# Letting a build-time scheduler choose the engine for copies, ReLUs, squares and adds, with the VectorE/GpSimd port in its clock

## The chip, the cores and the metric

The kernel runs on all 8 cores of one Trainium2 chip, each core working on 2 of the 16 sequences. The metric is the device time of the slowest core, in microseconds (us). A program on all 8 cores has a second, slower state in some executions, in which one die shows a lower granted TensorE clock; only fast runs are compared here. A ratio is the mean time of one kernel's fast runs over the mean of the fast runs of the kernel before, taken in the same rounds on the same chip. It is therefore not quite the ratio of the medians that are also quoted.

Engine names: PE is TensorE, DVE is VectorE, ACT is ScalarE, POOL is GpSimd, SP is SyncE.

## The reference

Two layers over a (16, 2048, 1024) stream. Layer 0 mixes with retention (6 heads of 128), layer 1 with causal forgetting attention (12 heads of 64). Both add 4 heads of attention to 256 memory tokens, an output projection, and a squared-ReLU MLP, each between two RMS norms.

```python
def reference(x, mem, ...):                       # cut to its structure
    for i in range(2):
        h = rmsnorm(x, g_pre_mix[i])
        proj = h @ w_in[i]                        # q | k | v | (gate or forget logits) | memory-q
        self_out = retention(...) if i == 0 else forgetting_attention(...)
        mem_out = memory_attention(mq, mem, g_mem[i], w_mem_kv[i])
        x = x + rmsnorm(concatenate([self_out, mem_out], -1) @ w_out[i], g_post_mix[i])
        h = rmsnorm(x, g_pre_mlp[i])
        u = relu(h @ w_up[i])
        x = x + rmsnorm((u * u) @ w_down[i], g_post_mlp[i])
    return x
```

## The kernel before

The kernel is written as many small generator tasks, and a list scheduler runs once, at build time. It keeps a clock for each engine and, at each step, advances the task that can go first. So the order of every engine's instructions is fixed at build time from modelled costs, and any change to the model reorders all engines.

```python
class Sched:
    def add(self, eng, fn, reads=(), writes=(), ..., cost=100.0):
        ...                                        # cut: dependencies become semaphores
        t = self.avail[eng]
        for d in keep:
            t = max(t, d.end + HOP)                # HOP = 160 ns between engines
        op.cost = cost
        op.end = t + cost
        ...
        self.avail[eng] = op.end                   # cut: DMAs have another rule

class Tasks:
    def run(self):
        while self.live:
            now = S.avail["pe"]
            for t in self.live:                    # in order of rank
                ...
                r = S.ready(*p) + (SLACK if p[0] == "pe" else 0.0)
                if r <= now + SOON: best = t; break
                if best is None or r < best_r: best, best_r = t, r
            self.step(best)
```

The engine of each operation was written by hand. The places that the change touches (cut):

```python
def seam(...):                                     # residual add after a norm, 8 chunks
    stt(t.ap, hb.ap[:, c, :], gcol(gi, l, c), rs.ap, ALU.mult, ALU.mult, ...)          # DVE -> tb
    tt(xs[c].ap, xs[c].ap, t.ap, ALU.add, ..., eng=("pool" if c % 2 else "dve"))
def square(...):   act(sq.ap, src, AF.Square, [srcR], [sq.R])
def v_proj(...):   act(dst, o3, AF.Copy, ...) if n % 2 else cp(dst, o3, ...)           # cp is DVE
def rope(...):     tt(dst.ap, t1.ap, swp.ap, ALU.add, ..., eng="pool")                 # the rope add
def head_end(...): tt(mix[:, h, :], rs.ap, sg.ap, ALU.mult, ..., eng="pool")           # retention product
def fin(...):      tt(mix[:, p, :], o_.ap, r.ap, ALU.mult, ..., eng="pool")            # attention product
def evac(hb, oc, bk, sm):                          # after the output projection
    cp(hb.ap[:, oc, :], bk.ap, [bk.R], [hb.R[oc]])                                     # DVE
    act(sq.ap, bk.ap, AF.Square, [bk.R], [sq.R])
def mlp_job(...):
    act(r.ap, bk.ap, AF.Relu, [bk.R], [r.R])
    tt(u2[:, i, :], r.ap, r.ap, ALU.mult, [r.R], [u2R[i]])                             # u square, DVE
```

The kernel divides PSUM, the memory that matmuls write their results to, into 8 banks; 3 of them (called `G` in the code) serve all projections and the whole MLP, so the next group of 8 to 32 matmuls waits until a copy, ReLU or product has emptied one of the three.

The softmax here doesn't subtract the row's maximum and nothing guards it: scores larger than these inputs give would overflow.

## Time and profile before

| | before |
|---|---|
| median of 40 runs | 3601.12 us |
| fastest | 3589.0 us |
| PE, DVE, ACT, POOL busy | 92%, 54%, 49%, 18% |

From the page of the kernel before (slowest core, 7): busy time of each engine with its share and its count; the clock granted to PE in 40 slices, in tenths; the chain that ended last, by engine.

```profile
...
PE 3308.0 (92%) x16476; PEld 1537.4 (43%) x16476; DVE 1947.4 (54%) x3273; ACT 1773.0 (49%) x3173; POOL 661.4 (18%) x708
...
PEclk9789999999999999999999999999999999999998
...
PE 77%; DMA 7%; DVE 7%; issue 5%; ACT 3%; SPq 1%; POOL 1%; DVEq 0%; ACTq 0%; POOLq 0%
...
```

PE is the bound. Its clock dips (7 and 8 tenths) in the second and third slice and in the last. But "92% busy" contains modelled ends of matmuls, so a better reading is the spacing. The table of engine busy time in two stretches of the MLP, kernel before (from:to in us; length; then busy time and count of PE, PEld, DVE, ACT, POOL; granted clock, DMA share, GB/s):

```profile
...
3330.00:3420.00 90.00, 90.00 (x418) 40.79 (x417) 38.55 (x63) 25.07 (x42) 10.73 (x10) 1.00 0.61 193
3420.00:3510.00 90.00, 90.00 (x418) 40.83 (x417) 18.47 (x39) 22.35 (x38) 1.33 (x3) 1.00 0.38 122
...
```

418 matmuls of 512 columns in 90 us is 215 ns each, with a granted clock of 1.00: PE's full rate here. DVE and ACT are mostly idle here; there is nothing to gain in these stretches.

For the rest of this document *PE loss* means this: over all consecutive matmul starts, the spacing less what the first one's columns take at the full clock, (columns x 0.4167 + 2) ns, summed, plus the time before the first matmul and that after the last. The formula is a fit to the trace, where back-to-back matmuls start 215 to 216 ns apart at 512 columns, 162 to 163 at 384 and 56 at 128. It is worked out from the trace, as a mean over the six cores whose matmul records are complete. Stages are cut where a stage's first value-projection matmul is issued.

| PE loss, us | first block | rest of 1st retention | 1st forgetting | 2nd retention | 2nd forgetting | after the last output projection | sum |
|---|---|---|---|---|---|---|---|
| before | 112.9 | 72.7 | 86.0 | 52.8 | 44.7 | 37.8 | 407 |

The cores spread by 0.5 to 5 us in a column (standard deviation). 56 of the 407 us are matmuls that ran at half clock after a gap (427 ns apart at 512 columns); 351 us are gaps.

Groups of DVE instructions of the kernel before (line, engine, operation, names, shapes, count | busy us, mean ns | idle before, with what ended it):

```profile
...
L624 DVE TENSOR_TENSOR u_s<-rb_s 128x512 bf16<-128x512 bf16 x512 | 247.5, 484 | 507.0 <-ACT rb_s L615 506.0
...
L624 DVE TENSOR_TENSOR xt_s<-xt_s,tb_s 128x512 f32<-128x512 f32 x128 | 121.7, 950 | 28.1 <-DVE tb_s L627 11.4 <-DMA xt_s<-xs 10.7
L636 DVE CAST hb_s<-pb 128x512 bf16<-128x512 f32 x144 | 99.2, 690 | 128.3 <-PE pb L604 127.5
...
L624 DVE TENSOR_TENSOR un_s<-pb,un_s 128x512 f32<-128x512 f32 x96 | 65.9, 687 | 35.1 <-PE pb L604 31.5 <-DMA un_s<-rot 2.7
...
```

The residual add (`xt_s<-xt_s,tb_s`) averages 950 ns, while operations of the same 512 columns that read PSUM (`pb`) take 687 to 690 ns. In the trace of core 7, 84 of the 128 adds have no POOL operation beside them and take 693 ns, and 44 have one and take 1443 ns on average. This lengthening beside POOL is called a *port hold*, or hold, below. The list of waits of the kernel before, all engines (waiting engine, line and tile <- releaser: us in total, times, longest):

```profile
...
ACT sq_s L615 <- DVE hb_s L636: 232.0, 134, 5.0
...
DVE un_s L636 <- DMA vcache<-un_s: 93.3, 18, 13.2
...
ACT un_s L615 <- DMA vcache<-un_s: 65.8, 12, 10.1
...
```

ACT's square of an output bank waits for DVE's copy of the same bank (232 us); copies of values wait for the store of the previous values (93 and 66 us).

### The profile page before, as it was taken

To read this page: it belongs to the slowest core of one execution; us is meant where nothing else is said; L and a number is where in the kernel's file an instruction comes from. 1 tells how busy PE (TensorE), PEld (TensorE's weight loads), DVE (VectorE), ACT (ScalarE), POOL (GpSimd) and SP (SyncE) were. 2 spreads that over 40 slices of the span, in tenths; PEclk is the share of its full clock that TensorE was granted. 3 is DMA by queue.
4 is the path that set the end of the run, shared out by engine and by line. 5 is a ranking of instruction groups with operands and counts; after the bars stand their busy time and mean duration, and the time that the engine had idled before them with its cause. 6 is when DMAs were issued, how large, how long until landed. Compare 5 with 4: busy or idle time off the path is not lost.

```text
span 3590.2 us, 57714 instructions; the slowest of 8 cores (3567.0 to 3590.2 us)
## 1 busy us (share of the span) xinstructions
PE 3308.0 (92%) x16476; PEld 1537.4 (43%) x16476; DVE 1947.4 (54%) x3273; ACT 1773.0 (49%) x3173; POOL 661.4 (18%) x708
## 2 busy tenths in 40 slices
PE   5688999898999898999999999999999989999996
PEld 2234444443444343443444444444444444444442
DVE  4666766465544534436666666666665453524514
ACT  3544444354732484874444444444575358586221
POOL 1222322111102101011222212231111101102102
PEclk9789999999999999999999999999999999999998
DMA  9779885876346848466653655355565453634534
GB/s 185 173 222 219 225 241 173 199 212 206 115 162 176 212 133 214 111 172 208 190 190 103 200 194 181 123 184 179 161 196 158 154 173 106 188 95 144 183 120 164
DMA packets 271411, 623.27 MB, mean 174 GB/s; under 512 B 54912, under 2 KB 66816, under 8 KB 271104
## 3 DMA queue, kind: packets, MB, share of 16 engines
q1 hardware_dynamic: 220928, 449.70, 39.4%
q0 software_dynamic: 50176, 169.89, 19.8%
q8 instruction: 143, 2.34, 0.3%
q14 instruction: 164, 1.34, 0.2%
HBM read 505.08 MB, written 168.56 MB: 188 GB/s over the span
## 4 chain that ended last, share of the span: by engine, by line
PE 77%; DMA 7%; DVE 7%; issue 5%; ACT 3%; SPq 1%; POOL 1%; DVEq 0%; ACTq 0%; POOLq 0%
PE pb L604 76%; DMA vcache<-un_s 2%; DMA wm_s<-wall 2%; DVE un_s L624 1%; DVE tb_s L627 1%; SPq L639 1%; ACT sq_s L615 1%; DMA wf_s<-wall 1%; DVE un_s L643 1%; DVE sq_s L624 1%; DVE xt_s L624 1%; ACT rs_s L615 1%; DMA xt_s<-xT 0%; POOL un_s L624 0%; DMA xt_s<-xs 0%
## 5 line engine op out<-in xcount | busy, mean ns | idle before, releaser
L604 PE MATMUL pb<-u_s,wf_s 128*128 128x512 bf16 x4096 | 995.4, 382 | 35.9 <-DVE un_s L636 13.7
L604 PE MATMUL pb<-hb_s,wf_s 128*128 128x512 bf16 x4096 | 966.2, 383 | 35.0 <-ACT rb_s L615 8.5
L615 ACT ACTIVATE pt_s<-pb,dcol_s 128x512 bf16<-128x512 f32 x960 | 561.4, 624 | 118.4 <-PE pb L604 99.9
L604 PEld LDWEIGHTS pb<-hb_s,wf_s 128*128 128x128 bf16 x4096 | 399.6, 99 | 513.1 <-issue 70.7
L604 PE MATMUL pb<-hb_s,wm_s 128*128 128x512 bf16 (+1 forms) x2240 | 586.4, 387 | 32.1 <-DVE un_s L624 13.1
L604 PEld LDWEIGHTS pb<-u_s,wf_s 128*128 128x128 bf16 x4096 | 396.3, 98 | 487.4 <-issue 57.7
L624 DVE TENSOR_TENSOR u_s<-rb_s 128x512 bf16<-128x512 bf16 x512 | 247.5, 484 | 507.0 <-ACT rb_s L615 506.0
L615 ACT ACTIVATE rb_s<-pb 128x512 bf16<-128x512 f32 x512 | 304.6, 596 | 439.0 <-PE pb L604 363.8
L604 PE MATMUL pb<-un_s 65*128 65x512 bf16 (+5 forms) x1536 | 405.1, 303 | 10.5 <-DVE rs_s L624 2.4
L615 ACT ACTIVATE sq_s<-xt_s 128x512 bf16<-128x512 f32 (+1 forms) x400 | 235.2, 610 | 270.9 <-DVE xt_s L624 221.5
L604 PE MATMUL pb<-pt_s,un_s 128*128 128x512 bf16 x960 | 326.9, 346 | 0.0
L604 PEld LDWEIGHTS pb<-hb_s,wm_s 128*128 128x128 bf16 (+1 forms) x2240 | 211.0, 99 | 265.4 <-issue 66.4
L624 POOL TENSOR_TENSOR xt_s<-xt_s,tb_s 128x512 f32<-128x512 f32 x128 | 178.3, 1393 | 630.5 <-DVE tb_s L627 609.7
L636 DVE CAST un_s<-pb 64x512 bf16<-64x512 f32 (+1 forms) x256 | 167.4, 654 | 232.5 <-PE pb L604 129.3
L624 DVE TENSOR_TENSOR un_s<-pb,un_s 128x512 f32<-128x512 f32 (+2 forms) x336 | 231.0, 687 | 61.9 <-PE pb L604 31.5
L615 ACT ACTIVATE sq_s<-pb 128x512 bf16<-128x512 f32 x192 | 114.6, 597 | 268.1 <-DVE hb_s L636 232.0
L604 PE MATMUL pb<-mix_s,wm_s 128*128 128x512 bf16 x1024 | 239.4, 384 | 7.7 <-ACT sq_s L615 4.6
L636 DVE COPY rs_s<-pb 64x512 f32<-64x512 f32 x192 | 132.1, 688 | 196.2 <-PE pb L604 121.1
L624 DVE TENSOR_TENSOR sq_s<-sq_s 128x512 bf16<-128x512 bf16 (+1 forms) x408 | 189.4, 477 | 80.5 <-ACT sq_s L615 77.6
L572 POOL DMA_DIRECT2D wm_s<-wbf x154 | 87.0, 565 | 773.6 <-PE pb L604 753.7
L604 PE MATMUL pb<-wm_s,hb_s 128*128 128x384 bf16 x1024 | 195.8, 337 | 25.5 <-DVE un_s L636 10.2
L627 DVE SCALAR_TENSOR_TENSOR tb_s<-hb_s,cst_s,rs_s 128x512 f32<-128x512 bf16 x256 | 196.2, 779 | 22.8 <-ACT rs_s L615 22.8
(70 smaller groups left out, 2788.5 us busy)
## 6 DMA issues: line engine op xcount, KB each, us to landing
wf_s<-wbf SPq DMA_DIRECT2D x224, 512.0 KB, 4.2
wm_s<-wbf POOLq DMA_DIRECT2D x133, 768.0 KB, 6.3
xs<-xt_s SPq DMA_DIRECT2D x192, 256.0 KB, 4.5
xt_s<-xs SPq DMA_DIRECT2D x192, 256.0 KB, 6.7
xt_s<-xT SPq DMA_DIRECT2D x128, 256.0 KB, 8.3
wf_s<-wall POOLq DMA_DIRECT2D x64, 512.0 KB, 8.3
wbf<-wf_s SPq DMA_DIRECT2D x64, 512.0 KB, 6.5
y<-xt_s SPq DMA_DIRECT2D x112, 256.0 KB, 3.7
```

What stands on the lines that cost most here:

```text
L572: S.add(self.eng, (lambda d_, s_: lambda e, sem: e.dma_start(out=d_, in_=s_).then_inc(sem, 16))(dst, src), reads=[wbR[key]], writes=[self. ...
L604: S.add("pe", lambda e: e.matmul(out, lhsT=lhsT, rhs=rhs, start=start, stop=stop, **kw), reads=reads, writes=writes, cost=c)
L615: S.add("act", lambda e: e.activation(out=out, in_=in_, func=func, **kw), reads=reads, writes=writes, cost=c + 0.833 * nfree(out))
L624: S.add(eng, lambda e: e.tensor_tensor(out=out, in0=in0, in1=in1, op=op), reads=reads, writes=writes, cost=vcost(eng, out, (in0, in1)))
L627: S.add(eng, lambda e: e.scalar_tensor_tensor(out=out, in0=in0, scalar=scalar, in1=in1, op0=op0, op1=op1), reads=reads, writes=writes, cos ...
L636: S.add(eng, lambda e: e.tensor_copy(out=out, in_=in_), reads=reads, writes=writes, cost=vcost(eng, out, (in_,)))
L639: S.add("sp", lambda e, sem: e.dma_start(out=out, in_=in_).then_inc(sem, 16), reads=reads, writes=writes, dma=True, dres=dres, nbytes=nbyt ...
L643: S.add(eng, lambda e: e.memset(ap, v), reads=reads, writes=writes, cost=100 + 0.5 * nfree(ap))
```

## The change

The intent: give each of these operations to the engine that would finish it first on the scheduler's clock. It has three parts:

- **the ACT/DVE part**: copies out of PSUM, key scaling, ReLU and squares choose between ACT and DVE;
- **the POOL part**: residual adds, rope adds, products, square adds and casts choose between DVE and POOL (casts also ACT);
- **the port part**: the scheduler's clock treats the SBUF port that DVE and POOL share as one more resource. An operation with two SBUF inputs on either, or a POOL copy, starts no earlier than the last booking ends, and the choice weighs this too.

```diff
+        self.port = 0.0
...
+        if port:
+            t = max(t, self.port)
+            self.port = t + cost
...
+    def on_chip(*ins):
+        return len(ins) > 1 and not any("psum" in str(type(i.tensor)).lower() for i in ins)
+    def either(engs, cost, reads, writes, port=()):
+        return min(engs, key=lambda e: max(S.ready(e, reads, writes), S.port if e in port else 0.0) + cost[e])
+    def evacuate(out, in_, reads, writes, engs=("dve", "act")):
+        e = either(engs, {...}, reads, writes, ("pool",))
+        ...                                        # act(... AF.Copy ...) or cp(..., eng=e)
+    def tt_any(out, in0, in1, op, reads, writes):
+        e = either(("dve", "pool"), {"dve": vcost(...), "pool": vcost(...) + POOLB}, reads, writes, ("dve", "pool"))
+        tt(out, in0, in1, op, reads, writes, eng=e)
...
-            tt(xs[c].ap, xs[c].ap, t.ap, ALU.add, ..., eng=("pool" if c % 2 else "dve"))
+            tt_any(xs[c].ap, xs[c].ap, t.ap, ALU.add, ...)
-        cp(hb.ap[:, oc, :], bk.ap, [bk.R], [hb.R[oc]])
+        evacuate(hb.ap[:, oc, :], bk.ap, [bk.R], [hb.R[oc]])
-                    act(r.ap, bk.ap, AF.Relu, [bk.R], [r.R])
+                    if either(("act", "dve"), {"act": 700.0, "dve": 800.0}, [bk.R], [r.R]) == "dve":
+                        ts(r.ap, bk.ap, 0.0, None, ALU.max, None, [bk.R], [r.R])
+                    else:
+                        act(r.ap, bk.ap, AF.Relu, [bk.R], [r.R])
...                                                # cut: fourteen more places of the same kinds, and port=... in tt, stt and cp
```

More of the change, by code (lines that the diff above doesn't have):

```diff
@@ L94, in ready, with add @@
         return t
-    def add(self, eng, fn, reads=(), writes=(), dma=False, ndma=1, dres=None, final=False, cost=100.0, nbytes=0, ncast=0):
+    def add(self, eng, fn, reads=(), writes=(), dma=False, ndma=1, dres=None, final=False, cost=100.0, nbytes=0, ncast=0, port=False):
         op = Op()
@@ L232 @@
 SOON = 60.0
+POOLB = 300.0
 class Buf:
@@ L621, in vcost, with squared @@
         return 125 + (0.62 if out.dtype == BF and all(i.dtype == BF for i in ins) else 1.1) * n
+    def on_chip(*ins):
[3 more added lines that the diff above has]
+    def evacuate(out, in_, reads, writes, engs=("dve", "act")):
+        e = either(engs, {"dve": vcost("dve", out, (in_,)), "act": 172 + 0.833 * nfree(out), "pool": vcost("pool", out, (in_,))}, reads, writes, ("pool",))
+        if e == "act":
+            act(out, in_, AF.Copy, reads, writes)
+        else:
+            cp(out, in_, reads, writes, eng=e)
+    def squared(out, in_, reads, writes):
+        if either(("act", "dve"), {"act": 700.0, "dve": 900.0}, reads, writes, ("dve",)) == "dve":
+            tt(out, in_, in_, ALU.mult, reads, writes)
+        else:
+            act(out, in_, AF.Square, reads, writes)
+    def tt_any(out, in0, in1, op, reads, writes):
+        e = either(("dve", "pool"), {"dve": vcost("dve", out, (in0, in1)), "pool": vcost("pool", out, (in0, in1)) + POOLB}, reads, writes, ("dve", "pool"))
+        tt(out, in0, in1, op, reads, writes, eng=e)
     def tt(out, in0, in1, op, reads, writes, eng="dve"):
-        S.add(eng, lambda e: e.tensor_tensor(out=out, in0=in0, in1=in1, op=op), reads=reads, writes=writes, cost=vcost(eng, out, (in0, in1)))
+        S.add(eng, lambda e: e.tensor_tensor(out=out, in0=in0, in1=in1, op=op), reads=reads, writes=writes, cost=vcost(eng, out, (in0, in1)),
+              port=on_chip(in0, in1))
     def stt(out, in0, scalar, in1, op0, op1, reads, writes, eng="dve"):
         S.add(eng, lambda e: e.scalar_tensor_tensor(out=out, in0=in0, scalar=scalar, in1=in1, op0=op0, op1=op1),
-              reads=reads, writes=writes, cost=50 + vcost(eng, out, (in0, in1, U_f)))
+              reads=reads, writes=writes, cost=50 + vcost(eng, out, (in0, in1, U_f)), port=on_chip(in0, in1))
     def ts(out, in0, s1, s2, op0, op1, reads, writes, eng="dve"):
@@ L635, in cp @@
     def cp(out, in_, reads, writes, eng="dve"):
-        S.add(eng, lambda e: e.tensor_copy(out=out, in_=in_), reads=reads, writes=writes, cost=vcost(eng, out, (in_,)))
+        S.add(eng, lambda e: e.tensor_copy(out=out, in_=in_), reads=reads, writes=writes, cost=vcost(eng, out, (in_,)), port=eng == "pool")
     def spdma(out, in_, reads, writes, dres, nbytes, **kw):
@@ L721, in sq_into @@
             a = sm.acc[sm.n % 2]
-            tt(a.ap, a.ap, sq.ap, ALU.add, [a.R, sq.R], [a.R])
+            tt_any(a.ap, a.ap, sq.ap, ALU.add, [a.R, sq.R], [a.R])
             sq.busy = False
@@ L728, in square @@
         yield ("act", [srcR], [sq.R])
-        act(sq.ap, src, AF.Square, [srcR], [sq.R])
+        squared(sq.ap, src, [srcR], [sq.R])
         if free is not None:
@@ L770, in seam @@
             stt(t.ap, hb.ap[:, c, :], gcol(gi, l, c), rs.ap, ALU.mult, ALU.mult, [hb.R[c], rs.R, cstR], [t.R])
-            tt(xs[c].ap, xs[c].ap, t.ap, ALU.add, [xs[c].R, t.R], [xs[c].R], eng=("pool" if c % 2 else "dve"))
+            tt_any(xs[c].ap, xs[c].ap, t.ap, ALU.add, [xs[c].R, t.R], [xs[c].R])
             t.busy = False
@@ L943, in mem_q @@
             yield from group(bk, lambda k: wu[u][:, k, :], lambda k: h.ap[:, k, :], lambda k: [wR, h.R[k]])
-            act(mix[:, 6 + u, :], bk.ap, AF.Copy, [bk.R], [mixR[6 + u]])
+            evacuate(mix[:, 6 + u, :], bk.ap, [bk.R], [mixR[6 + u]])
             bk.busy = False
@@ L1036, in v_proj @@
                     dst, w_ = vs.ap[:, :, 0:3:2, :], [vs.R]
-                if n % 2:
-                    act(dst, o3, AF.Copy, [bk.R], w_)
-                else:
-                    cp(dst, o3, [bk.R], w_)
+                evacuate(dst, o3, [bk.R], w_)
                 bk.busy = False
@@ L1071, in rest @@
             yield (e_, [t1.R, swp.R], [dst.R])
-            tt(dst.ap, t1.ap, swp.ap, ALU.add, [t1.R, swp.R], [dst.R], eng=e_)
+            tt_any(dst.ap, t1.ap, swp.ap, ALU.add, [t1.R, swp.R], [dst.R])
             if b == 0:
                 f0 = (qf0 if name == "q" else kf0)[hs.ap]
-                tt(f0.ap, t1.ap[:, 0:128], swp.ap[:, 0:128], ALU.add, [t1.R, swp.R], [f0.R], eng=e_)
+                tt_any(f0.ap, t1.ap[:, 0:128], swp.ap[:, 0:128], ALU.add, [t1.R, swp.R], [f0.R])
             t1.busy = False
@@ L1088, in rest @@
                 yield ("dve", [tb.R], [kt.R])
-                ts(kt.ap, tv, kd, None, ALU.mult, None, [tb.R, cstR], [kt.R])
+                if either(("dve", "act"), {"dve": 450.0, "act": 690.0}, [tb.R], [kt.R]) == "dve":
+                    ts(kt.ap, tv, kd, None, ALU.mult, None, [tb.R, cstR], [kt.R])
+                else:
+                    act(kt.ap, tv, AF.Copy, [tb.R, cstR], [kt.R], scale=kd)
                 tb.busy = False
@@ L1219, in head_end @@
             ob.busy = False
-            tt(mix[:, h, :], rs.ap, sg.ap, ALU.mult, [rs.R, sg.R], [mixR[h]], eng="pool")
+            tt_any(mix[:, h, :], rs.ap, sg.ap, ALU.mult, [rs.R, sg.R], [mixR[h]])
             rs.busy = sg.busy = False
@@ L1312, in fox_qk @@
         for hh in range(2):
-            cp(qs[hh].ap[0:64, :], bk.ap[64 * hh:64 * hh + 64, :], [bk.R], [qs[hh].R[0]])
+            evacuate(qs[hh].ap[0:64, :], bk.ap[64 * hh:64 * hh + 64, :], [bk.R], [qs[hh].R[0]])
         bk.busy = False
@@ L1327, in fox_qk @@
         for hh in range(2):
-            cp(ks[hh].ap[0:64, bsl(b)], bk.ap[64 * hh:64 * hh + 64, :], [bk.R], [ks[hh].R[b]])
+            evacuate(ks[hh].ap[0:64, bsl(b)], bk.ap[64 * hh:64 * hh + 64, :], [bk.R], [ks[hh].R[b]])
         bk.busy = False
@@ L1362, in fin @@
             act(r.ap, r.ap, AF.Exp, [r.R], [r.R], scale=-1.0)
-            tt(mix[:, p, :], o_.ap, r.ap, ALU.mult, [o_.R, r.R], [mixR[p]], eng="pool")
+            tt_any(mix[:, p, :], o_.ap, r.ap, ALU.mult, [o_.R, r.R], [mixR[p]])
             r.busy = o_.busy = False
@@ L1384, in pv @@
                         o_ = yield from rsB.acq()
-                    cp(r.ap[p0:p0 + 64, :], ob.ap[q0:q0 + 64, :], [ob.R], [r.R])
-                    cp(o_.ap[p0:p0 + 64, :], ob.ap[p0:p0 + 64, :], [ob.R], [o_.R])
+                    evacuate(r.ap[p0:p0 + 64, :], ob.ap[q0:q0 + 64, :], [ob.R], [r.R])
+                    evacuate(o_.ap[p0:p0 + 64, :], ob.ap[p0:p0 + 64, :], [ob.R], [o_.R])
                     ob.busy = False
@@ L1482, in y_part @@
         x = yield from xB.acq()
-        if t:
-            yield ("dve", [bk.R], [x.R])
-            cp(x.ap, bk.ap, [bk.R], [x.R])
-        else:
-            yield ("act", [bk.R], [x.R])
-            act(x.ap, bk.ap, AF.Copy, [bk.R], [x.R])
+        yield ("act" if S.avail["act"] < S.avail["dve"] else "dve", [bk.R], [x.R])
+        evacuate(x.ap, bk.ap, [bk.R], [x.R])
         bk.busy = False
@@ L1499, in y_whole @@
         yield ("act", [x.R], [sq.R])
-        act(sq.ap, x.ap, AF.Square, [x.R], [sq.R])
+        squared(sq.ap, x.ap, [x.R], [sq.R])
         K.spawn(sq_into(sm, sq), 0)
@@ L1503, in y_whole @@
         yield (e_, [x.R], [hb.R[oc]])
-        cp(hb.ap[:, oc, :], x.ap, [x.R], [hb.R[oc]], eng=e_)
+        evacuate(hb.ap[:, oc, :], x.ap, [x.R], [hb.R[oc]], ("dve", "act", "pool"))
         x.busy = False
@@ L1531, in mlp_job @@
                     r = yield from rB.acq()
-                    act(r.ap, bk.ap, AF.Relu, [bk.R], [r.R])
+                    if either(("act", "dve"), {"act": 700.0, "dve": 800.0}, [bk.R], [r.R]) == "dve":
+                        ts(r.ap, bk.ap, 0.0, None, ALU.max, None, [bk.R], [r.R])
+                    else:
+                        act(r.ap, bk.ap, AF.Relu, [bk.R], [r.R])
                     bk.busy = False
```

## The prediction

> **What bounds it now.** TensorE. The page's busy table gives PE 3308 us of 3590 (92%), DVE 54%, ACT 49%, POOL 18%; the chain of waits is 77% PE. In the MLP stretch at 3330-3510 us the stage table shows 418 matmuls per 90 us, 215 ns each; spacing all matmuls at that rate leaves an estimated 370 us of PE loss, 282 us of it visible as idle. Where it lies matters: about 128 us in the first 360 us, about 58 us at 360-720, about 73 us in the second retention stage (1620-2520), about 60 us in the four starts of forgetting attention (near 700, 880, 1200, 1390 us), where copies wait for the value-cache stores, and almost none in MLP stretches. By the list of waits PE waits some 215 us for DVE, ACT or POOL and 32 us for DMA; of the first, about 95 us fall before 360 us and about 63 us in the other retention stretches.
>
> **What the port costs now.** The Trainium skill, "SBUF — State Buffer", section "SBUF: two separate sides", says a VectorE operation with two SBUF inputs and a GpSimd operation exclude each other for their whole length. This trace agrees: DVE's residual add takes 693 ns (median) with no POOL operation beside it and 1443 ns (mean of 44) with one; the u square 426 and 962; copies and adds that read PSUM take 687 either way. Summed over the groups, DVE is held an estimated 120 us.
>
> **What the change does** (the instruction order shows it). POOL's arithmetic falls from 456 to 53 operations: all 128 residual adds, all 96 mix products, 84 of 96 rope adds and 87 of 112 casts leave it, most to DVE. To ACT go 136 of 144 output copies, 76 query/key copies, 39 key scalings, 37 value copies; to DVE come 99 of 512 ReLUs and 23 squares. Costed with this trace's durations (0.69 us per DVE add or PSUM copy, 0.60 per ACT copy), DVE gains about 330 us and loses about 210 us, plus about 110 us of the port holds: DVE stays near 1950 us. ACT rises by about 125 us to near 1900; POOL falls to about 200 us, mostly DMA issue.
>
> **How much is on the critical path.** Little. PE's own work is unchanged. Rope adds and mix products get shorter (1.3 to 0.7 us), holds of 0.5 to 3 us inside DVE's queue go, so retention and startup waits should shrink by about a third: (95+63)/3, about 50 us. Not helped: weight loads at startup (DMA 70-92% busy up to 540 us), value-cache stores, MLP. The seams gain nothing: a pair of chunks takes 3.0 us now (timeline of the tail); all on DVE it is 2x(0.74+0.17+0.69)=3.2 us. So the last 25 us after the last matmul stay.
>
> **Predicted:** 3545 us, range 3485 to 3605. Faster by over 2%: 0.30; within 2%: 0.66; slower by over 2%: 0.04.
>
> **What would show each step.** Residual add back at 693 ns with hardly a 1.4 us case, u square mean near 430; DVE busy 1900-2000, ACT 1850-1950, POOL 150-250; PE busy about the same, PE idle 220-250; the gain before 720 us and in 1620-2520, none in MLP stretches; value-cache waits still there.
>
> **What would make it wrong.** Startup waits that are really DMA-bound leave only 20 us; ACT queues during forgetting attention (already 80 of 90 us busy at 1260-1350) make PE wait for query/key copies; the reordered PE stream, all of which moves, may shift the stage overlap by 1% either way; if more of the small gaps between matmuls (90 us) came from port holds, the gain passes 2%.

## More of the kernel before

PE's own waits on core 7, second retention stage (1700 to 2490 us) of the kernel before:

```profile
...
PE pb L604 <- DVE un_s L624: 6.3, 6, 2.2
PE pb L1084 <- POOL un_s L624: 5.2, 5, 2.2
PE pb L604 <- DVE un_s L636: 3.7, 2, 3.1
PE pb L604 <- ACT rb_s L615: 3.5, 3, 1.4
...
```

and in the second forgetting-attention stage (2490 to 3280 us):

```profile
...
PE pb L604 <- DVE un_s L636: 7.0, 1, 7.0
PE pb L604 <- ACT rb_s L615: 5.5, 1, 5.5
PE pb L604 <- DVE un_s L632: 4.3, 2, 2.4
...
```

## The result, and the profile after

The changed kernel takes 3571.35 us (median of 20 runs; before 3601.12, 40 runs); the ratio of fast runs is 0.9929, with a 95% interval of 0.9919 to 0.9939. That is a gain of 0.7%, clear of noise, and a little under half of the 1.5% that was predicted.

The page of the changed kernel (slowest core, 6):

```profile
...
PE 3282.9 (92%) x16155; PEld 1536.3 (43%) x16476; DVE 1958.5 (55%) x3463; ACT 1890.8 (53%) x3386; POOL 200.3 (6%) x305
...
PEclk9789999999999999999999999999999999999998
...
PE 75%; DMA 10%; DVE 7%; issue 4%; ACT 3%; SPq 1%; DVEq 0%; ACTq 0%; POOL 0%; POOLq 0%; another core or an unknown queue 0%
...
```

PE is still 75% of the chain and the clock dips at the same place. The missing PE records (16155 of 16476) are records, not work. DVE stayed where it was, ACT rose by 118 us, POOL fell to 200 us. The same two stretches of the MLP, changed kernel:

```profile
...
3330.00:3420.00 90.00, 89.58 (x410) 40.79 (x417) 27.95 (x52) 23.30 (x39) 0.00 (x0) 1.00 0.58 179
3420.00:3510.00 90.00, 89.58 (x410) 40.82 (x417) 22.74 (x49) 25.31 (x42) 0.00 (x0) 1.00 0.38 120
...
```

PE's weight loads (417 in 90 us, one for each matmul) say what the incomplete matmul records can't: the full rate, as before. The DVE groups of the changed kernel:

```profile
...
L656 DVE TENSOR_TENSOR u_s<-rb_s 128x512 bf16<-128x512 bf16 x512 | 218.0, 426 | 395.8 <-ACT rb_s L620 383.5 <-DVE rb_s L665 0.5
...
L656 DVE TENSOR_TENSOR xt_s<-xt_s,tb_s 128x512 f32<-128x512 f32 x256 | 177.3, 693 | 41.5 <-DVE tb_s L660 26.8 <-DMA xt_s<-xs 3.9 <-DMA xt_s<-xT 0.2
...
L656 DVE TENSOR_TENSOR un_s<-pb,un_s 128x512 f32<-128x512 f32 x96 | 66.1, 688 | 32.7 <-PE pb L609 31.3 <-DMA un_s<-rot 0.6
...
L669 DVE CAST hb_s<-pb 128x512 bf16<-128x512 f32 x8 | 5.5, 690 | 11.3 <-PE pb L609 11.3
...
```

Twice as many residual adds, each at 693 ns; the port holds are gone. The list of waits of the changed kernel, all engines:

```profile
...
ACT un_s L620 <- DMA vcache<-un_s: 123.6, 27, 14.3
...
DVE un_s L669 <- DMA vcache<-un_s: 46.8, 9, 13.4
...
ACT sq_s L620 <- DVE hb_s L669: 2.3, 4, 0.8
...
```

The square no longer waits for DVE's copy: both are on ACT now. The waits for value stores have not gone; more of them sit on ACT. PE's waits on core 7 in about the second retention stage (1700 to 2490 us), changed kernel:

```profile
...
PE pb L609 <- DVE un_s L656: 18.4, 17, 2.3
PE pb L609 <- DVE sq_s L656: 6.9, 3, 5.0
PE pb L609 <- DMA mkv_s<-memkv: 4.5, 2, 2.3
PE pb L609 <- ACT rb_s L620: 3.6, 4, 1.6
...
```

PE waits more for DVE here than before (18.4 us for `un_s`, products and adds of the rotary step, against 6.3 and 5.2 us). In the second forgetting-attention stage (2490 to 3280 us), changed kernel:

```profile
...
PE pb L609 <- DVE un_s L665: 3.9, 2, 2.0
PE pb L609 <- ACT un_s L620: 3.9, 4, 1.8
PE pb L609 <- DVE mix_s L656: 1.7, 1, 1.7
...
```

The 7.0 and 5.5 us waits of before are gone. The loss by stage says the same for all cores:

| PE loss, us | first block | rest of 1st retention | 1st forgetting | 2nd retention | 2nd forgetting | after | sum |
|---|---|---|---|---|---|---|---|
| before | 112.9 | 72.7 | 86.0 | 52.8 | 44.7 | 37.8 | 407 |
| changed | 111.7 | 77.7 | 68.5 | 63.9 | 28.8 | 33.0 | 384 |
| difference | -1.2 | +5.0 | -17.5 | +11.1 | -15.9 | -4.8 | -23 |

So the gain came in forgetting attention, and retention *lost* 15 us.

PE's waits in the first 360 us, slowest core, kernel before (core 7):

```profile
...
PE pb L604 <- DVE sq_s L624: 29.6, 10, 14.9
PE pb L604 <- ACT sbf_s L615: 23.2, 13, 4.6
...
PE pb L604 <- DMA wm_s<-wall: 8.3, 4, 3.6
...
```

and changed kernel (core 6):

```profile
...
PE pb L609 <- DVE sq_s L656: 21.3, 7, 14.3
PE pb L609 <- DMA mkv_s<-memkv: 17.0, 1, 17.0
PE pb L609 <- ACT sbf_s L620: 14.0, 15, 3.4
...
```

Summed over these lists and averaged over the eight cores, PE's waits for DVE, ACT and POOL in the first 360 us fell from 86.9 to 76.8 us, and its waits for DMA rose from 15.0 to 26.0 us, above all by one wait for the load of the memory keys and values (`mkv_s<-memkv`). In the other two windows of the prediction, waits for engines rose: from 27.1 to 31.9 us at 360 to 720 us, and from 34.5 to 36.1 us at 1620 to 2520 us.

### The profile page after: what moved, and what is told of

Same layout as the page of the kernel before. It is cut to its first block, busy times and chain, and to the rows that moved or that the text cites. A ratio compares the mean times of both kernels' runs of the same rounds, so it can differ in the third digit from the quotient of the medians.

```text
span 3570.5 us, 56485 instructions; the slowest of 8 cores (3546.4 to 3570.5 us)
## 1 busy us (share of the span) xinstructions
PE 3282.9 (92%) x16155; PEld 1536.3 (43%) x16476; DVE 1958.5 (55%) x3463; ACT 1890.8 (53%) x3386; POOL 200.3 (6%) x305
## 4 chain that ended last, share of the span: by engine, by line
PE 75%; DMA 10%; DVE 7%; issue 4%; ACT 3%; SPq 1%; DVEq 0%; ACTq 0%; POOL 0%; POOLq 0%; another core or an unknown queue 0%
PE pb L609 75%; DVE un_s L656 3%; DMA vcache<-un_s 3%; DMA mkv_s<-memkv 2%; DMA wf_s<-wall 2%; SPq L672 1%; DVE tb_s L660 1%; DVE un_s L676 1%; ACT rs_s L620 1%; DVE xt_s L656 1%; DMA wbf<-wf_s 1%; DMA xt_s<-pos 1%; DMA wm_s<-wbf 0%; DMA wm_s<-wall 0%; DVE hb_s L660 0%
## 5 line engine op out<-in xcount | busy, mean ns | idle before, releaser
L609 PE MATMUL pb<-u_s,wf_s 128*128 128x512 bf16 x4007 | 974.7, 381 | 34.5 <-DVE un_s L656 12.8
L609 PE MATMUL pb<-hb_s,wm_s 128*128 128x512 bf16 (+1 forms) x2175 | 573.3, 386 | 23.6 <-DVE un_s L656 12.8
L620 ACT ACTIVATE rb_s<-pb 128x512 bf16<-128x512 f32 x413 | 246.5, 597 | 419.1 <-PE pb L609 342.7
L656 DVE TENSOR_TENSOR u_s<-rb_s 128x512 bf16<-128x512 bf16 x512 | 218.0, 426 | 395.8 <-ACT rb_s L620 383.5
L609 PE MATMUL pb<-pt_s,un_s 128*128 128x512 bf16 (+3 forms) x924 | 315.8, 345 | 0.1
L620 ACT ACTIVATE un_s<-pb 128x384 bf16<-128x384 f32 (+2 forms) x225 | 122.8, 546 | 319.8 <-PE pb L609 183.6
L656 DVE TENSOR_TENSOR sq_s<-sq_s 128x512 bf16<-128x512 bf16 (+1 forms) x398 | 163.9, 420 | 198.7 <-ACT sq_s L620 195.6
L656 DVE TENSOR_TENSOR un_s<-pb,un_s 128x512 f32<-128x512 f32 (+2 forms) x336 | 231.1, 688 | 52.8 <-PE pb L609 31.3
L609 PEld LDWEIGHTS pb<-un_s 65*128 65x128 bf16 (+2 forms) x1536 | 141.4, 100 | 148.7 <-issue 22.3
L656 DVE TENSOR_TENSOR xt_s<-xt_s,tb_s 128x512 f32<-128x512 f32 x256 | 177.3, 693 | 41.5 <-DVE tb_s L660 26.8
L669 DVE CAST un_s<-pb 64x512 bf16<-64x512 f32 (+1 forms) x143 | 94.8, 663 | 182.4 <-PE pb L609 130.5
```

Of the source, the lines that this page charges most:

```text
L609: S.add("pe", lambda e: e.matmul(out, lhsT=lhsT, rhs=rhs, start=start, stop=stop, **kw), reads=reads, writes=writes, cost=c)
L620: S.add("act", lambda e: e.activation(out=out, in_=in_, func=func, **kw), reads=reads, writes=writes, cost=c + 0.833 * nfree(out))
L656: S.add(eng, lambda e: e.tensor_tensor(out=out, in0=in0, in1=in1, op=op), reads=reads, writes=writes, cost=vcost(eng, out, (in0, in1)), po ...
L669: S.add(eng, lambda e: e.tensor_copy(out=out, in_=in_), reads=reads, writes=writes, cost=vcost(eng, out, (in_,)), port=eng == "pool")
```

## The experiments

Eighteen kernels ran, with five rounds each. "Loss" figures are the means of the table at the end of this section; the expectations quote medians, a few us lower. The kernels of one heading shared one chip and its runs of the kernel before. The chips differ: the kernel before took 3607.9 us on that of the second set (mean of fast runs) and 3595.0 to 3599.9 us on those of the first, third and fourth.

### First set: the parts, with the port in the clock

Theory 1 was the prediction's: taking work off POOL ends the holds, and that is the gain. Theory 2: the ACT/DVE choices are the gain. Theory 3: any reshuffle of the order would do as much.

**e_bal**: the POOL part undone.
```diff
-            tt_any(xs[c].ap, xs[c].ap, t.ap, ALU.add, ...)
+            tt(xs[c].ap, xs[c].ap, t.ap, ALU.add, ..., eng=("pool" if c % 2 else "dve"))
...                    # likewise rope adds, products, square adds, casts
```

> The ACT/DVE choices of the change, with the port in the clock, but all of POOL's arithmetic kept on POOL as before. Theory 1 (the gain comes from taking work off POOL and so ending the port holds): ratio to before 0.998 to 1.002, the residual add near 950 ns on average, forgetting-attention loss of PE near 125 us as before. Theory 2 (the gain comes from choosing between ACT and DVE in the forgetting-attention layer, the POOL move costs time in retention): ratio 0.985 to 0.993, forgetting-attention loss near 95 us although the residual add is still held to some 950 ns, retention loss not above before's 237 us. Theory 3 (only the reshuffled order counts): anything within 1%, in any stage.

Measured: ratio 1.0014 (0.9972 to 1.0057). No gain, and the forgetting-attention loss is 123.9 us (before 130.7): outside theory 2's range and inside theory 1's.

**e_pool**: the ACT/DVE part undone.
```diff
-        evacuate(hb.ap[:, oc, :], bk.ap, [bk.R], [hb.R[oc]])
+        cp(hb.ap[:, oc, :], bk.ap, [bk.R], [hb.R[oc]])
...                    # likewise ten more places: ReLU, squares, key scaling, other copies
```

> Only POOL's arithmetic moved (residual adds, rope adds, mix products, casts, square adds), with the port in the clock; ACT/DVE copies, ReLUs and squares fixed as before. Theory 1: ratio 0.992 to 0.996, the residual add at 693 ns. Theory 2: ratio 0.999 to 1.006, holds gone all the same, retention loss up by 10 us or more, forgetting-attention loss near before's 125 us. Theory 3: anything within 1%.

Measured: ratio 1.0060 (0.9996 to 1.0124; two fast runs only). DVE groups of e_pool:

```profile
...
L656 DVE TENSOR_TENSOR u_s<-rb_s 128x512 bf16<-128x512 bf16 x512 | 217.0, 424 | 456.8 <-ACT rb_s L620 455.9
...
L656 DVE TENSOR_TENSOR xt_s<-xt_s,tb_s 128x512 f32<-128x512 f32 x256 | 177.2, 692 | 45.0 <-DVE tb_s L660 24.9 <-DMA xt_s<-xs 8.8
...
```

The holds are all but gone (692 and 424 ns), and the time is not better. So theory 1 falls by this run as theory 2 did by the last: neither half pays alone, as long as the port is in the clock.

**e_port**: both parts undone, the port stays in the clock, every operation on its old engine.

> Only the port in the scheduler's clock; every operation on its old engine. Theories 1 and 2: ratio 0.998 to 1.002, holds as before (residual add near 950 ns). Theory 3: as likely 0.7% off as the change itself.

Measured: ratio 1.0096 (1.0046 to 1.0146). None of the theories had a 1% cost here. The list of PE's waits, e_port, core 7, 3300 to 3350 us, the seam after the last output projection:

```profile
...
PE pb L609 <- DVE sq_s L656: 14.4, 2, 12.2
...
```

and the kernel before, core 7, around the same seam (3255 to 3350 us):

```profile
...
PE pb L604 <- DVE sq_s L624: 0.8, 1, 0.8
```

PE stands 12.2 us at one norm matmul (on the sums of squares; the list names the releasing DVE tile). By the timeline of the trace, PE had issued all that came before it at 3332 us, and the seam's adds and squares, on which the norm waits, ran from 3325 to 3346 us; in the kernel before the same seam was done in time. No operation had changed engine, so the order alone made this. In this stage e_port lost 56.4 us, the kernel before 37.8. e_bal and e_pool both carry this clock, with 51.2 and 49.5 us here; against e_port they are 0.8% and 0.4% faster (the ratios divided; the 0.4% is within the noise of e_pool's two fast runs).

**e_hop**: control; the kernel before with another hop time.
```diff
-HOP = 160.0
+HOP = 165.0
```

> Control for reshuffling: the kernel before with one number of the scheduler's clock changed (the hop between engines 165 ns and not 160), so that the order moves and nothing else. Theories 1 and 2: ratio 0.998 to 1.002. Theory 3: a change of 0.4% or more in either direction.

Measured: 0.9983 (0.9919 to 1.0047), and the loss by stage within 6 us of before in every column. The order does move: at 3277 of the 16476 places in core 3's sequence of matmuls, one of other tiles stands. The mean is far from 0.7%, but with three fast runs the interval does not exclude it; theory 3 is not supported, and not ruled out by this run alone.

### Second set: without the port in the clock

**b_bal**: the ACT/DVE part alone; POOL part and port part undone.
```diff
-        if port:
-            t = max(t, self.port)
-            self.port = t + cost
...                    # and the POOL part as in e_bal
```

> The kernel before with the ACT/DVE choices alone: POOL's arithmetic on POOL, and no port in the scheduler's clock. Separates the two things that the first run of that name joined. If the port in the clock is what spoiled it there (alone it cost 1.0%), this is faster than before: ratio 0.989 to 0.995, forgetting-attention loss of PE near 100 us (before 129), the waits of the norm matmuls (those on the sums of squares) small. If the ACT/DVE choices gain only when POOL is emptied as well: 0.998 to 1.004.

Measured: 0.9932 (0.9918 to 0.9945), the whole gain of the change from one of its three parts. The loss in forgetting attention hardly moved (127.3); second retention fell from 52.8 to 28.2 us, while the rest of the first retention layer rose from 72.7 to 84.4 us (part of this may be the slower chip). PE's waits of b_bal on core 7, 1700 to 2490 us, where the rotary step's 6.3 and 5.2 us of before are down to 3.8:

```profile
...
PE pb L606 <- DVE un_s L653: 3.8, 5, 1.2
PE pb L606 <- DVE sq_s L653: 3.6, 3, 1.7
...
```

and, from its list of all waits (232.0 us before):

```profile
...
ACT sq_s L617 <- DVE hb_s L666: 3.6, 5, 1.7
...
```

With copy and square of an output bank on the same engine, that wait has gone.

**a_noport**: the whole change, less the port part.
```diff
-        if port:
-            t = max(t, self.port)
-            self.port = t + cost
```

> The whole change with the port left out of the scheduler's clock and so out of the choice (53 of 96 rope adds and 55 of 112 casts then stay on POOL, residual adds and products go to DVE all the same). If the port model is what makes the change work: 0.998 to 1.005 against before, with norm-matmul waits of 15 us or more. If the model is only a cost and the moves do the work: 0.985 to 0.993, no slower than the change (0.993).

Measured: 0.9873 (0.9855 to 0.9891), faster than the change. DVE and ACT are about as busy as in the change; POOL is busier (316.8 against 200.3 us):

```profile
...
PE 3293.1 (93%) x16476; PEld 1534.7 (43%) x16476; DVE 1961.0 (55%) x3387; ACT 1874.1 (53%) x3356; POOL 316.8 (9%) x411
...
```

The port model is a cost here. Second retention loses 38.0 us, against 63.9 with the port (another chip) or 57.0 (a_hop below, this chip).

**a_rope**: the change, with rope adds kept on POOL.
```diff
-            tt_any(dst.ap, t1.ap, swp.ap, ALU.add, [t1.R, swp.R], [dst.R])
+            tt(dst.ap, t1.ap, swp.ap, ALU.add, [t1.R, swp.R], [dst.R], eng=e_)
```

> The whole change with the rope adds put back on POOL, everything else chosen as in the change. If the rope adds on DVE are what took retention's gain away by making DVE's queue longer and PSUM banks free later: retention loss of PE falls from 253 to 238 us or less, ratio to before 0.986 to 0.991. If port holds matter more: some operations are held again, retention loss stays or rises, ratio 0.993 to 1.000.

Measured: 0.9922 (0.9868 to 0.9975). Second retention improved to 48.3 us, but all retention stages together stayed at 248.6 (changed: 253.3), and the ratio is that of the change. One of the four runs counted as fast (3607.1 us) had one die at a clock of 0.956 to 0.961; without it the ratio is 0.990. Inconclusive: pinning an operation on POOL may also bring e_port's trouble with the clock back, which was not tested.

**a_hop**: control; the change with the hop at 165 ns.

> Control: the change with the hop at 165 ns and not 160. If the change's gain is its own and not one order's luck: ratio to before 0.990 to 0.996, forgetting-attention loss again near 97 us and retention near 250. If luck: it falls anywhere within 1% of before, and the losses by stage scatter by 15 us or more.

Measured: 0.9912 (0.9890 to 0.9933), as expected: forgetting attention 103.3, retention 255.0 us (two fast runs). Two orders of the change give the same gain, which speaks against the luck of one order.

### Third set: which moves pay

**b_pool0**: the POOL part alone, no port.

> The kernel before with the POOL work free to move and nothing else: no port in the scheduler's clock, ACT/DVE copies fixed as before. With the ACT/DVE choices at 0.993 and both without the port at 0.987, additive parts give 0.994. If moving POOL's work helps only where ACT has taken copies off DVE: 0.998 to 1.004, retention loss above before's by 10 us or more.

Measured: 1.0007 (0.9988 to 1.0026). DVE groups of b_pool0:

```profile
...
L653 DVE TENSOR_TENSOR u_s<-rb_s 128x512 bf16<-128x512 bf16 x512 | 232.6, 455 | 484.3 <-ACT rb_s L617 482.0 <-ACT mkv_s L617 1.3
...
L653 DVE TENSOR_TENSOR xt_s<-xt_s,tb_s 128x512 f32<-128x512 f32 x256 | 186.6, 729 | 43.7 <-DVE tb_s L657 24.9 <-DMA xt_s<-xs 7.1
...
```

The residual add averages 729 ns, nearly free of holds, and nothing is gained: DVE is busier (57%; 252 of POOL's 456 operations have moved) and second retention rises to 60.7 us. So the parts are not additive. POOL's work pays only where ACT has taken copies off DVE: on top of b_bal (0.9932) it brings 0.6% more (a_noport, 0.9873, the same chip).

**n_xt**: as a_noport, with every second residual add back on POOL.
```diff
-            tt_any(xs[c].ap, xs[c].ap, t.ap, ALU.add, ...)
+            tt(xs[c].ap, xs[c].ap, t.ap, ALU.add, ..., eng=("pool" if c % 2 else "dve"))
```

> Both parts without the port in the clock, but every second residual add back on POOL, so that its port holds return (residual add on DVE near 950 ns on average, u square held again). If ending the holds is worth what was predicted for it: slower than without this edit (0.9873) by 0.4% or more, ratio 0.991 to 0.996. If the holds lie off the path: 0.985 to 0.990.

Measured: 0.9952 (0.9922 to 0.9982; two fast runs). DVE groups of n_xt (DVE's durations are what is read):

```profile
...
L653 DVE TENSOR_TENSOR u_s<-rb_s 128x512 bf16<-128x512 bf16 x512 | 254.9, 498 | 432.9 <-ACT rb_s L617 419.3 <-PE pb L606 1.3
...
L653 DVE TENSOR_TENSOR xt_s<-xt_s,tb_s 128x512 f32<-128x512 f32 x128 | 128.1, 1001 | 32.0 <-DVE tb_s L657 11.0 <-DMA xt_s<-xT 7.5 <-DMA xt_s<-xs 7.5
...
```

The holds are back (1001 and 498 ns), and the gain falls from 1.3% to 0.5%. Once the copies are balanced, the residual adds on DVE are worth about 0.8% (0.7% against n_rr on the same chip). Where, the undisturbed die of n_xt's profile tells: cores 5, 6 and 7 lose 46 us in second forgetting attention and 37 after the last output projection, where a_noport and n_rr lose 30 and 31 to 33. The prediction had counted nothing for either stage. Holds and the adds' own placement were not separated.

**n_rr**: as a_noport, with rope adds and retention's products kept on POOL.

> Both parts without the port in the clock, with the rope adds and retention's mix products kept on POOL and only residual adds, forgetting-attention products and casts free to move. If DVE's queue in retention is what the POOL move costs there: second-retention loss from 38 us to near 28, ratio 0.982 to 0.986, the fastest so far. If not: 0.986 to 0.990.

Measured: 0.9881 (0.9862 to 0.9899). Not the fastest, a miss: second retention did fall, from a_noport's 38.0 to 33.0 us, but the rest of the first retention layer rose from 79.0 to 83.4.

**b_mlp**: the ACT/DVE choice for the MLP's ReLUs, squares and partial sums. The edit also frees the squares of the residual stream in the seams, since they share one function, so it is a little more than the MLP.

> The kernel before with the ACT/DVE choice in the MLP alone (ReLU, squares, partial-sum copies). If the gain of the ACT/DVE choices comes from the mixer's copies, above all the 136 output copies that go to ACT beside their squares: ratio 0.998 to 1.001. If from freeing PSUM banks of the MLP sooner: 0.993 to 0.996.

Measured: 0.9973 (0.9955 to 0.9991), between the two ranges: about 0.3% of b_bal's 0.7% comes from these choices. The mixer's copies alone were not run; the remaining 0.4% is a difference between two jobs.

### Fourth set: what the port part costs

**re_after**: the change again, on this chip.

> The change itself again, as the reference on this chip: ratio to before 0.991 to 0.995.

Measured: 0.9939 (0.9918 to 0.9960). The order of the matmuls is the same as in the first trace, and the losses by stage are those of that trace, to within 2 us.

**n_hop**: the change without the port part, with the hop at 165 ns.

> The change without the port in the clock, with the hop at 165 ns and not 160. If leaving the port out is worth 0.6% whatever the order: ratio 0.985 to 0.990. If the earlier 0.9873 was one order's luck: 0.990 to 0.996.

Measured: 0.9863 (0.9847 to 0.9878). Without the port the same chip gives 0.8% less time than the change (3546.1 against 3573.1 us, means of five fast runs each). But n_hop differs from the change in the hop too. At one hop, across chips, the port costs 0.5 to 0.7% (0.9873 against 0.9929 and 0.9939; 0.9863 against 0.9912); on the second set's chip, with another hop, 0.4% (a_noport against a_hop, whose intervals just touch). So 0.4 to 0.8%, with two orders on either side.

**a_choice**: the port weighs in the choice, but delays nothing on the clock.
```diff
-            t = max(t, self.port)
-            self.port = t + cost
+            self.port = max(t, self.port) + cost
```

> The change with the port only weighed when an engine is chosen; no operation is delayed by it on the clock. If the delays on the clock are what costs: 0.985 to 0.990, with second-retention loss near 40 us. If the different choice (84 rope adds on DVE and not 43) is what costs: as the change, 0.991 to 0.995, loss near 60 us.

Measured: 0.9945 (0.9929 to 0.9960), with 65.1 us in second retention. Taking the delays off the clock gives nothing back, so in the change it is the choices made with the port that cost. (In e_port, where nothing is chosen, it can only be the delays.)

**a_fill**: the port booked as intervals; a later-recorded operation may use a gap.
```diff
-            t = max(t, self.port)
-            self.port = t + cost
+            t = self.slot(t, cost)              # the first gap of `held` that is long enough
+            self.held = sorted(self.held + [(t, t + cost)])[-400:]
...                                              # and the choice asks slot() too
```

> The change with the port booked as intervals, so that a later-recorded operation may use a gap before an already booked one. If the cost is that the port is booked in recorded order: 0.985 to 0.990. If a port model of any kind costs, because the chip hardly holds operations once POOL is nearly empty: 0.991 to 0.995.

Measured: 0.9900 (0.9886 to 0.9915), at the edge of the first range and below the second: about half of the cost comes back (re_after 0.9939, n_hop 0.9863). Booking the port in recorded order is a part of the cost and not the whole. Here it was the first layer that improved (68.8 us in the rest of first retention), not second retention (61.8), though as many rope adds sit on DVE (83 large ones, 84 in the change).

### Fifth set: the rope adds

**n_rdve**: no port, all rope adds on DVE.

> No port in the clock, all 96 rope adds (and the 24 small ones) on DVE, casts and square adds chosen as without the port. If the rope adds on DVE are what the port's choice costs: second-retention loss 57 to 66 us, ratio to before 0.991 to 0.995. If it is the casts and square adds: loss near 40 us, ratio 0.985 to 0.989.

Measured: 0.9978 (0.9931 to 1.0026). In its profiled run, counted as fast, one die stood at a lower clock (cores 6 and 7 at 0.958) and took longer. On the other die its cores have a median of 3569 us, and those of n_rpool, in the same job, 3538 us. Second retention lost 47.0 us, not 57 to 66: the guess that rope adds on DVE make the loss of *that* stage has fallen.

**n_rpool**: no port, all rope adds on POOL.

> No port in the clock, all rope adds on POOL, the rest chosen as without the port. If rope adds on DVE cost: second-retention loss 28 to 38 us, ratio 0.984 to 0.988, the best or equal to the best. If it is the other moves: near 40 us, 0.985 to 0.989. The two theories differ little here; this run is for the better version.

Measured: 0.9878 (0.9855 to 0.9901), no better than leaving the choice free; second retention 47.8 us. All rope adds on DVE cost 0.9% on the undisturbed die (3569 against 3538 us, one profiled run each), half of them cost nothing. On this die the cost lies in the first retention layer: 204 us of loss there (first block and rest) for n_rdve, 173 for n_rpool; second retention is equal to within about 1 us.

### All losses by stage

| PE loss, us | ratio | first block | 1st ret. | 1st forg. | 2nd ret. | 2nd forg. | after | sum |
|---|---|---|---|---|---|---|---|---|
| before | 1 | 112.9 | 72.7 | 86.0 | 52.8 | 44.7 | 37.8 | 407 |
| e_hop | 0.9983 | 112.0 | 68.7 | 86.9 | 51.2 | 50.4 | 38.3 | 408 |
| e_port | 1.0096 | 107.9 | 88.6 | 75.2 | 67.6 | 46.5 | 56.4 | 442 |
| e_bal | 1.0014 | 115.1 | 86.6 | 84.5 | 43.0 | 39.4 | 51.2 | 420 |
| e_pool | 1.0060 | 109.9 | 74.2 | 88.9 | 69.5 | 44.4 | 49.5 | 436 |
| changed | 0.9929 | 111.7 | 77.7 | 68.5 | 63.9 | 28.8 | 33.0 | 384 |
| a_hop | 0.9912 | 116.0 | 82.0 | 67.6 | 57.0 | 35.7 | 32.7 | 391 |
| a_choice | 0.9945 | 111.6 | 79.7 | 71.1 | 65.1 | 27.3 | 32.1 | 387 |
| a_fill | 0.9900 | 111.8 | 68.8 | 65.9 | 61.8 | 28.7 | 32.5 | 370 |
| a_rope | 0.9922 | 117.2 | 83.1 | 78.7 | 48.3 | 28.7 | 33.0 | 389 |
| b_bal | 0.9932 | 118.0 | 84.4 | 87.9 | 28.2 | 39.4 | 37.8 | 396 |
| b_mlp | 0.9973 | 113.5 | 80.9 | 75.9 | 37.7 | 50.4 | 38.7 | 397 |
| b_pool0 | 1.0007 | 112.4 | 81.3 | 83.0 | 60.7 | 37.8 | 37.9 | 413 |
| a_noport | 0.9873 | 117.5 | 79.0 | 82.5 | 38.0 | 29.7 | 32.8 | 380 |
| n_hop | 0.9863 | 113.0 | 72.8 | 66.3 | 43.3 | 29.8 | 32.6 | 358 |
| n_rr | 0.9881 | 115.5 | 83.4 | 78.5 | 33.0 | 29.7 | 31.4 | 372 |
| n_rpool | 0.9878 | 107.1 | 72.1 | 86.6 | 47.8 | 30.5 | 32.5 | 377 |

The losses come from one profiled run each, on different chips, so differences of 5 us between sets mean little, and the rows of the second set (b_bal, a_noport, a_rope, a_hop) hold an estimated 10 us more than the others, by the time of the kernel before on that chip. Compare them with each other first. (n_xt and n_rdve, with their slower dies, and re_after, which repeats the change, are left out.)

## Why the prediction was right or wrong

**Right: what bounds it.** PE, at full rate in the MLP stretches, before and after (417 weight loads per 90 us in both, one for each matmul), with nothing gained there.

**Right: the port holds and the sums of busy time.** The residual add went to 693 ns and the u square to 426. DVE 1958 us (predicted near 1950), ACT 1891 (near 1900), POOL 200 (about 200). The value-cache waits stayed, as predicted: 159 us before, 170 after (sums of the two lines shown). One sum was off: PE's idle time, predicted at 220 to 250 us, is 252 to 264 us on the cores with complete records.

**Nearly right: the tail.** The prediction gave it nothing; the stretch after the last output projection, the final MLP job included, gave 5 us.

**Wrong: the term "retention and startup waits should shrink by about a third: (95+63)/3, about 50 us".** The loss of the first block went from 112.9 to 111.7, of the rest of the first retention layer from 72.7 to 77.7, of the second from 52.8 to 63.9: 15 us more, not 50 us less. The gain that did come, 38 us, was in the two forgetting-attention layers (33 us) and the tail (5 us), for which the prediction counted nothing. In the prediction's own windows, the startup waits for engines did shrink, by 10 us and not by a third of 95, but waits for DMA grew by 11 us in the same 360 us: the prediction had named this danger ("startup waits that are really DMA-bound"). The retention waits for engines grew by 6 us. That the DMA waits took the startup gain is read from the traces; no run isolates it. Net, 23 us of loss, 0.6% of the time, near the measured 0.7%. The step reasoned that an operation that gets shorter (1.3 to 0.7 us) and holds that vanish shorten PE's waits. The runs showed three things in its place. All eight combinations of the three parts were run (ratio to the kernel before on the same chip):

| | without the port part | with it |
|---|---|---|
| neither part | 1 | 1.0096 (e_port) |
| POOL part | 1.0007 (b_pool0) | 1.0060 (e_pool) |
| ACT/DVE part | 0.9932 (b_bal) | 1.0014 (e_bal) |
| both | 0.9873 (a_noport) | 0.9929 (the change) |

1. *Ending the holds by moving POOL's work to DVE buys nothing by itself* (b_pool0 1.0007, residual add 729 ns; e_pool 1.0060, all holds but a few gone, and 0.4% less than e_port, within noise). The likely reason: a hold had kept DVE busy, and the moved work fills the same time: DVE's busy time was predicted unchanged, and with it its queue should have been too.
2. *The ACT/DVE choices pay alone* (b_bal 0.9932; 0.7 to 1.3% wherever the table lets one compare). They were counted as load only. With them, the POOL part pays another 0.6% (a_noport), and putting the residual adds back costs 0.8% (n_xt), most of it in second forgetting attention and after the last output projection. What the prediction said of these adds was "The seams gain nothing".
3. *The port in the clock takes 0.4 to 0.8% away again* (a_noport and n_hop, 0.9873 and 0.9863, against 0.9929, 0.9939 and 0.9912), and 0.5 to 1.0% in the other rows of the table. The prediction looked at the port on the chip and not at what a port in the scheduler's clock does to the choices. Taking the delays off the clock did not help (a_choice 0.9945); booking the port with usable gaps gave about half of it back (a_fill 0.9900).

Without the port part the change is worth 1.3%, close to the predicted 1.5%; the forecast total was thus near what the moves can give, but for another reason than the one stated. That is a coincidence and does not confirm the step.

**What stays open.** Which of the port's choices cost it. Rope adds were suspected: all of them on DVE do cost about 0.9%, but not in the stage where the change loses, and the change has 84 of 96 there. Casts and square adds were not tried one by one; the change puts 28 of the 112 casts on ACT, a_noport none. That PSUM banks come free sooner is argued from which matmuls wait, not isolated by a run. Also, every run reorders all engines: the controls moved 0.1 to 0.3% (none clear of noise), so differences of that size between variants are not explained here.

**The better version.** The change without the port part runs at 0.9873, and at 0.9863 with the other hop; both beat the kernel before and the change.

## What to carry to other kernels

When a scheduler fixes order from a modelled clock, a resource added to the model is also a change of every order and every choice: test the kernel with the model alone and with the moves alone, before crediting either. Balance the two engines that empty PSUM first, and only then fill the room this leaves with work from a slower engine; the second step bought nothing without the first. And time saved inside an engine's queue is worth counting only after asking what else the same change puts into that queue.

## What the Trainium skill lacked or had wrong

- "SBUF — State Buffer", section "SBUF: two separate sides": it says the loser of the shared port blocks for the other's whole operation. The traces agree: residual add 693 ns alone, 1443 ns (mean of 44) beside a POOL operation; operations with a PSUM input 687 ns either way. What the page lacks is that removing such holds can be worth nothing: in b_pool0 the residual add averages 729 ns and not 950, and the time is the same (1.0007).
- "TensorE: Matmul & The Clock Gate", Part 1: it advises to budget 13/16 of the clock for dense matmul on all cores. In the fast run of the kernel before, all eight cores ran the MLP stretches at 3330 to 3510 us at a granted clock of 1.00, 215 ns per 512 columns. The slowest run of the kernel before took 4132.5 us, with one die at 0.802 to 0.804. So both states occur, and the page, which tells of the lower clock only, does not say when an all-core run is spared it.
- No page says how much a kernel's time moves when only the order of its instructions does: 0.1 to 0.3%, not clear of noise, for a 5 ns change of a scheduler's constant (e_hop, a_hop, n_hop), 1.0% for a resource added to its clock with no operation moved (e_port).
